# Decoder trunk on one core: delays of the mixer steps chosen anew, and VectorE and ScalarE held behind each weight unit's split

## The chip, the core and the metric

One core of a Trainium2 chip. The metric is the device time of one execution in microseconds (us); smaller is better. The core has TensorE (PE in the profile), VectorE (DVE), ScalarE (ACT), GpSimd (POOL), and SyncE (SP), whose queue here issues most DMAs. Each engine works through its own instructions in the order in which they were written for it, and waits on semaphores for the others.

## The reference

Two layers of a hybrid decoder, for 256 tokens of width 2048, in float32. Of each layer this matters:

```python
proj = rms_norm(h, norm_w[l]) @ w_in[l]
y_a = deltanet_branch(dn_qkv, dn_z, dn_b, dn_a, ...)   # causal conv, SiLU, chunked delta rule, head norm, gate
y_b = hgrn2_branch(hg_q, hg_f, hg_i, ...)              # gated recurrence with one decay per channel, head norm, gate
h = h + concat([y_a, y_b]) @ w_out[l]
h = h + (p[l] @ w_ple_up[l]) * sigmoid(h @ w_ple_gate[l])
```

A final norm follows the second layer. Each branch has eight heads of 128, and the kernel treats them as four groups of two.

## The kernel before

**Weights.** All weight matrices are cut into about 390 units, in the order in which TensorE uses them: per layer the input projection (128 units), the output projection, the gate and the "up" projection. Units 0 to 127 are the input projection of layer 0, units 196 to 323 that of layer 1; unit 196+n of layer 1 corresponds to unit n. A unit comes by one DMA into a `raw` tile (five buffers). ScalarE writes its rounded part `whi` (L451), VectorE the rest, `wlo` = raw - whi (L453): this is the unit's split. `whi` and `wlo` have three buffers each, so the split of unit n needs the products of unit n-3 to be over. TensorE makes twelve matmuls of 128x512 per unit: whi times the high and the low part of the activations, and wlo times the high part (L389 is the helper for all matmuls). Tiles are named by kind, layer and group: `in1hi` is the projection that feeds layer 1's hg branch, and so on.

**The mixers.** Between the units' products, the two branches are computed as Python generators ("jobs"), one for each branch and group (`dn` delta rule, `hg` gated recurrence, `di` the triangular inverses for all dn groups). After the products of each unit, `run_step` calls `tick`, which counts every job down by one and lets those at zero emit their next step: some VectorE and ScalarE operations, a few small matmuls, DMAs. How many units pass between two steps is set by a number for each step, from the table `DELAY`, with exceptions for single groups in `DELAY_AT` (key: kind, group, step; the same for both layers). `yield self.wait("vq")` for dn group 0 waits `d0vq` units.

**What sets the order.** TensorE's instructions keep program order (`keep_in_program_order`). Those of VectorE, ScalarE and SyncE are put in order by the tile scheduler: among the instructions that its own model holds ready, the one that was written first goes first. `ahead(n)` writes the split of unit n+2 before the products of unit n, so a mixer operation that is written after a split can still be scheduled before it, if its operands are ready earlier.

**Names that recur below.** The hg branch needs factors for block sizes 2 to 128, `hg02X2` to `hg02X128` (layer 0, group 2): a VectorE subtraction for each half (L1211, L1213), one ScalarE exponential (L1216), a VectorE product with q (L1223). TensorE uses them in three lots: `hg02pa1` (sizes 1 to 8), `hg02pa16` (16, 32, 64), `hg02pa128`. `hg02fsg`, `hg02qsg`, `hg02k`, `hg02G`, `hg02Gk` are the gates, keys and sums of logarithms that come before them. In the dn branch, `dn10vac` is the convolved v, `dn10pvtr` its transposed copy, brought by a DMA on SP's queue, `dn10R` (L1070) the right-hand side made of it; `dn11zs` copies gate columns out of PSUM (L681). The inverse is built up by block size: `di1T`, `di1pp` (matmul), `di1P` (a ScalarE copy out of PSUM, L848 for size 64), `di1px` (matmul).

Of the kernel before, what the change touches and what calls it, by code (L numbers as in the profile page):

```python
# [8 lines left out]
F32 = mybir.dt.float32  # L9
# [3 lines left out]
AF = mybir.ActivationFunctionType  # L13
ALU = mybir.AluOpType
# [19 lines left out]
def chunk_cols(chunk):  # L34
# [152 lines left out]
def trunk(ctx: ExitStack, tc: tile.TileContext, head, xT, x, pT, W, par, fw, cst, msk, eye, out):  # L187
# [13 lines left out]
    V, S, G = nc.vector, nc.scalar, nc.gpsimd  # L201
# [236 lines left out]
    def prep(n):  # L438
# [11 lines left out]
        for sl in parts:  # L450
            S.activation(hi[:, sl], raw[:, sl], AF.Copy)  # L451
        for sl in parts:
            V.tensor_tensor(lo[:, sl], raw[:, sl], hi[:, sl].bitcast(F32), ALU.subtract)  # L453
# [1175 lines left out]
```

## Time and profile before

| | |
|---|---|
| runs, us | 1198.25, 1199.94, 1200.49 (median 1199.94) |
| the profiled execution, us | 1203.56 |
| its span, us | 1201.6 |
| mean granted TensorE clock | 0.996 |
| TensorE busy | 1183.9 us (99%) |
| VectorE, ScalarE busy | 868.6 (72%), 848.9 (71%) |
| DMA, mean | 221 GB/s |

Busy time is summed over the instructions of an engine. In the view of groups, one row holds all instructions of one line, operation and tile: busy time in all, the mean of one in ns, the engine's idle time just ahead of them, and what ended most of it. In the timeline a row gives start, duration, engine, line, operation, output and inputs, and in brackets the idle time before it with its releaser. A row that ends in xN holds N neighbouring instructions.

### The profile page before, as it was taken

What the parts mean: (1) busy time and instruction counts of PE and PEld (TensorE: products, weight loads), DVE (VectorE), ACT (ScalarE), POOL (GpSimd) and SP (SyncE); (2) the same over time, 40 slices, a digit from 0 to 9 for tenths busy, and PEclk for the clock granted to TensorE, in tenths of its full rate; (3) what the DMA queues carried; (4) which work ended last, traced back from release to release, by engine and by line L of the source; (5) the groups of instructions that cost most, each with busy time, mean ns of one, the idle gap of its engine ahead of it and who ended that gap; (6) DMA issues with size and microseconds to landing.
All of it is one profiled execution on the core that took longest, in us unless ns stands there. A gap on an engine that the chain in (4) does not pass through costs nothing.

```text
span 1201.6 us, 21188 instructions
## 1 busy us (share of the span) xinstructions
PE 1183.9 (99%) x7998; PEld 986.7 (82%) x7998; DVE 868.6 (72%) x1548; ACT 848.9 (71%) x1446; POOL 52.4 (4%) x52
## 2 busy tenths in 40 slices
PE   9999999999999999999999999999999999999997
PEld 8888888978788888888888888878777888888886
DVE  8569896889778655646765789786976786665565
ACT  7587887678787765547866888776876876665453
POOL 0000010001000000000000001000000000000010
PEclk9999999999999999999999999999998999999999
DMA  9589976596666659856978898757574675698562
GB/s 333 198 281 266 300 226 211 170 280 204 198 196 195 182 178 281 248 191 214 277 230 262 240 290 254 217 183 220 184 195 145 200 195 178 212 285 244 182 203 103
DMA packets 178006, 265.88 MB, mean 221 GB/s; under 512 B 107216, under 2 KB 114800, under 8 KB 177648
## 3 DMA queue, kind: packets, MB, share of 16 engines
q1 hardware_dynamic: 153792, 234.48, 64.1%
q10 hardware_dynamic: 24112, 30.06, 7.5%
q8 instruction: 62, 1.02, 0.4%
q14 instruction: 40, 0.33, 0.1%
HBM read 214.94 MB, written 27.02 MB: 201 GB/s over the span
## 4 chain that ended last, share of the span: by engine, by line
PE 66%; DVE 6%; ACT 5%; DMA 4%; issue 3%; SPq 1%; ACTq 0%; POOLq 0%; POOL 0%; DVEq 0%
PE out L389 15%; PE gate L389 14%; PE in1dk L389 7%; PE in1hf L389 7%; PE in1hi L389 6%; PE in0hf L389 3%; PE in0dv L389 3%; DVE wlo L453 2%; PE in1dv L389 2%; PE in0hi L389 2%; PE up L389 2%; ACT whi L451 2%; PE in1dz L389 1%; DMA dn10pvtr<-dn10pvd 1%; SPq L584 1%
## 5 line engine op out<-in xcount | busy, mean ns | idle before, releaser
L453 DVE TENSOR_TENSOR wlo<-raw,whi 128x1024 fp32r<-128x1024 f32 (+2 forms) x393 | 476.3, 1217 | 230.9 <-ACT whi L451 223.3
L451 ACT ACTIVATE whi<-raw 128x1024 fp32r<-128x1024 f32 (+2 forms) x393 | 407.8, 1044 | 204.0 <-PE out L389 59.4
L389 PE MATMUL in1hi<-whi,n1hi 128*128 128x512 f32 x128 | 41.2, 403 | 0.8 <-ACT dn11zs L681 0.8
L389 PE MATMUL in1hf<-whi,n1hi 128*128 128x512 f32 x128 | 40.7, 399 | 1.1 <-ACT hg11zs L681 1.1
L389 PE MATMUL in1dk<-whi,n1hi 128*128 128x512 f32 x128 | 39.8, 392 | 0.0
L389 PE MATMUL in1hi<-whi,n1lo 128*128 128x512 f32 x128 | 39.7, 391 | 0.0
L389 PE MATMUL in1hf<-whi,n1lo 128*128 128x512 f32 x128 | 39.5, 390 | 0.0
L389 PE MATMUL in1dk<-whi,n1lo 128*128 128x512 f32 x128 | 39.5, 390 | 0.0
L389 PE MATMUL gate<-whi,g0hi 128*128 128x512 f32 x128 | 39.4, 389 | 0.0
L389 PE MATMUL gate<-whi,g0lo 128*128 128x512 f32 x128 | 39.4, 389 | 0.0
L389 PE MATMUL in1hi<-wlo,n1hi 128*128 128x512 f32 x128 | 35.7, 391 | 1.8 <-DVE wlo L453 1.8
L389 PE MATMUL in1dv<-whi,n1hi 128*128 128x512 f32 (+1 forms) x128 | 37.4, 384 | 0.0
L389 PE MATMUL in1dv<-whi,n1lo 128*128 128x512 f32 (+1 forms) x128 | 35.8, 372 | 0.0
L389 PE MATMUL gate<-whi,g1lo 128*128 128x512 f32 (+1 forms) x120 | 35.7, 378 | 0.0
L389 PE MATMUL gate<-whi,g1hi 128*128 128x512 f32 (+1 forms) x120 | 35.7, 378 | 0.0
L389 PE MATMUL in1hf<-wlo,n1hi 128*128 128x512 f32 x128 | 35.6, 389 | 0.0
L389 PE MATMUL in1dk<-wlo,n1hi 128*128 128x512 f32 x128 | 35.6, 389 | 0.0
L389 PE MATMUL gate<-wlo,g0hi 128*128 128x512 f32 x128 | 35.5, 389 | 0.0
L389 PE MATMUL gate<-wlo,g1hi 128*128 128x512 f32 (+1 forms) x120 | 32.4, 378 | 0.0
L389 PE MATMUL in1dv<-wlo,n1hi 128*128 128x512 f32 (+1 forms) x128 | 32.3, 370 | 0.0
L389 PE MATMUL in0hi<-whi,n0hi 128*128 128x512 f32 x96 | 30.7, 401 | 0.0
L389 PE MATMUL in0hf<-whi,n0hi 128*128 128x512 f32 x96 | 30.1, 395 | 0.0
(1371 smaller groups left out, 2850.5 us busy)
## 6 DMA issues: line engine op xcount, KB each, us to landing
raw<-W SPq DMA_DIRECT2D x383, 512.0 KB, 4.2
raw<-W SPq DMA_DIRECT2D x7, 544.0 KB, 5.4
h<-x SPq DMA_DIRECT2D x4, 512.0 KB, 4.8
xt<-xT SPq DMA_DIRECT2D x3, 512.0 KB, 7.8
out_dram<-h SPq DMA_DIRECT2D x5, 256.0 KB, 2.4
dn00gall<-dn00d ACTq DMA_DIRECT2D x1, 1024.0 KB, 8.6
di0d<-di0Bt ACTq DMA_DIRECT2D x4, 256.0 KB, 4.5
dn10gall<-dn10d ACTq DMA_DIRECT2D x1, 1024.0 KB, 8.9
```

What stands on the lines that cost most here:

```text
L389: return tc.keep_in_program_order(nc.tensor.matmul(*a, **k))
L451: S.activation(hi[:, sl], raw[:, sl], AF.Copy)
L453: V.tensor_tensor(lo[:, sl], raw[:, sl], hi[:, sl].bitcast(F32), ALU.subtract)
L584: nc.sync.dma_start_transpose(u16(t).rearrange("p (k r) -> p k r", k=c // 128), d.rearrange("(r c) -> r c", c=c))
```

## The change

Two things. First, about 60 of the delays in `DELAY_AT` get other values. Second, a wrapper `Behind` stands in front of VectorE and ScalarE: every operation issued through it is tied, without a semaphore, behind the engine's last "mark", and `prep` sets that mark to the unit's split on this engine. So nothing that is written after the split of unit n can be scheduled ahead of it any more; what was written earlier may still come later. TensorE, GpSimd and SyncE are not wrapped. The instructions are the same in kind and number on every engine; only their order on VectorE, ScalarE and (for a few transfers) SyncE differs, and TensorE's order nearly not: the first half of `hg00pa1` and `hg10pa1` stands one unit earlier, `hg01po` one unit later. As all wrapped operations are issued from the wrapper, their line in the changed kernel is L211.

```diff
 DELAY_AT = {
-    "b0e": 8, "b0g": 3, "b0t": 7,
+    "b0e": 10, "b0g": 3, "b0t": 6,
...
-    "d0D": 6, "d0c": 6, "d0e": 3, "d0k": 4, "d0ke": 7, "d0qe": 3, "d0qt": 2, "d0ssq": 4, "d0v": 7, "d0vt": 3, "d0y": 2, "d0ye": 3, "d0yp": 5, "d0yt": 3, "d0z1": 4,
+    "d0D": 7, "d0c": 6, "d0e": 3, "d0k": 3, "d0ke": 6, "d0q": 8, "d0qe": 3, "d0qt": 2, "d0ssq": 5, "d0v": 7, "d0vq": 5, "d0vt": 3, "d0y": 2, "d0ye": 3, "d0yp": 6, "d0yt": 3, "d0z1": 4,
...
-    "h0a": 1, "h0e": 6, "h0f": 4, "h0o": 9, "h0s2": 3, "h0u16": 1, "h0u64": 2, "h0y": 7, "h0ye": 5, "h0yp": 7, "h0yt": 5,
+    "h0a": 1, "h0a2": 2, "h0e": 5, "h0f": 4, "h0o": 9, "h0s2": 3, "h0u16": 1, "h0u64": 2, "h0y": 4, "h0ye": 5, "h0yp": 8, "h0yt": 5,
...
-    V, S, G = nc.vector, nc.scalar, nc.gpsimd
+    class Behind:
+        def __init__(self, engine):
+            self.engine, self.mark = engine, None
+        def __getattr__(self, name):
+            op = getattr(self.engine, name)
+            def run(*a, **k):
+                i = op(*a, **k)
+                if self.mark is not None:
+                    tc.add_manual_dep(i.ins, self.mark, mybir.DependencyInfo(
+                        mybir.DependencyClass.NoSync, mybir.DependencyReason.DATA), reason="order")
+                return i
+            return run
+
+    V, S, G = Behind(nc.vector), Behind(nc.scalar), nc.gpsimd
...
         for sl in parts:
-            S.activation(hi[:, sl], raw[:, sl], AF.Copy)
+            S.mark = S.activation(hi[:, sl], raw[:, sl], AF.Copy).ins.name
         for sl in parts:
-            V.tensor_tensor(lo[:, sl], raw[:, sl], hi[:, sl].bitcast(F32), ALU.subtract)
+            V.mark = V.tensor_tensor(lo[:, sl], raw[:, sl], hi[:, sl].bitcast(F32), ALU.subtract).ins.name
```

**VectorE, layer 1, where `dn10R` stands.** The number behind `wlo` is the unit; numbers after an underscore are buffers. Before:

```order
L1211 TENSOR_TENSOR hg12X16_9758<-hg12G_9176,hg12Gk_9180 128x16x16 [waits PE_49]
L1213 TENSOR_TENSOR hg12X16_9758<-hg12G_9176 128x16x16
L453 TENSOR_TENSOR wlo294_9585<-raw294_9395,whi294_9584 128x1024 [waits DMAHW2_49,Activation_49]
L514 TENSOR_SCALAR hg12sz_9574<-hg12sz_9574 128x512 [waits Activation_49]
L1070 TENSOR_TENSOR dn10R_9781<-dn10pvtr_9532,invn_7275 128x512 [waits DMAHW1_49]
L1274 TENSOR_TENSOR hg12Ad_9534<-hg12pa1_9535,cs_90 128x128 [waits PE_49]
L453 TENSOR_TENSOR wlo295_9640<-raw295_9452,whi295_9639 128x1024 [waits DMAHW3_49,Activation_49]
L1240 COPY_PREDICATED hg12Ad_9534<-ms_91,hg12pa1_9535 128x64 [waits DVE_49]
L1223 TENSOR_TENSOR hg12X16_9758<-hg12X16_9758,hg12q_9127 128x16x16 [waits Activation_49]
```

and in the changed kernel:

```order
L211 SCALAR_TENSOR_TENSOR dn11vac_9781<-dn11vtr_9509,pr_89,dn11vac_9781 128x254 [waits DVE_49]
L211 TENSOR_TENSOR wlo298_9794<-raw298_9637,whi298_9793 128x1024 [waits DMAHW7_49,PE_49,Activation_49]
L211 SCALAR_TENSOR_TENSOR dn11vac_9781<-dn11vtr_9509,pr_89,dn11vac_9781 128x253 [waits DVE_49]
L211 TENSOR_TENSOR dn10R_9809<-dn10pvtr_9532,invn_7294 128x512 [waits DMAHW1_49]
L211 TENSOR_TENSOR wlo299_9816<-raw299_9693,whi299_9815 128x1024 [waits DMAHW2_49,PE_49,Activation_49]
L211 TENSOR_SCALAR dn11sg_9790<-dn11sg_9790 128x512 [waits Activation_49]
L211 TENSOR_TENSOR hg12X32_9868<-hg12G_9176,hg12Gk_9180 128x8x32
L211 TENSOR_TENSOR hg12X32_9868<-hg12G_9176 128x8x32
L211 TENSOR_TENSOR wlo300_9880<-raw300_9763,whi300_9879 128x1024 [waits DMAHW4_49,PE_49,Activation_49]
```

`dn10R` stood one place behind the split of unit 294, ahead of that of 295; now it stands between those of 298 and 299. The product and the subtractions for `hg12X16` and `hg12X32` have moved too: X16's subtractions from ahead of the split of 294 to behind that of 296.

**VectorE, layer 0, around the splits of units 94 to 97.** Before:

```order
L453 TENSOR_TENSOR wlo93_3191<-raw93_3017,whi93_3190 128x1024 [waits DMAHW5_49,PE_49,Activation_49]
L514 TENSOR_SCALAR dn00sg_3155<-dn00sg_3155 128x512 [waits Activation_49]
L1223 TENSOR_TENSOR hg02X4_3243<-hg02X4_3243,hg02q_2998 128x64x4
L453 TENSOR_TENSOR wlo94_3251<-raw94_3089,whi94_3250 128x1024 [waits DMAHW6_49,PE_49,Activation_49]
L1056 TENSOR_TENSOR dn00vac_3146<-dn00vac_3146,dn00sg_3155 128x512 [waits DVE_49,Activation_49]
L1223 TENSOR_TENSOR hg02X8_3329<-hg02X8_3329,hg02q_2998 128x32x8
L453 TENSOR_TENSOR wlo95_3337<-raw95_3163,whi95_3336 128x1024 [waits DVE_49,DMAHW7_49,PE_49,Activation_49]
L797 COPY_PREDICATED di0Tt_2168<-ms_91,di0px16_3206 32x16x16 [waits PE_49]
L797 COPY_PREDICATED di0Tt_2168<-ms_91,di0px16_3206 32x16x16 x3
```

and in the changed kernel:

```order
L211 TENSOR_TENSOR wlo94_3251<-raw94_3089,whi94_3250 128x1024 [waits DMAHW6_49,PE_49,Activation_49]
L211 COPY_PREDICATED di0Tt_2168<-ms_91,di0px16_3206 32x16x16 [waits PE_49]
L211 TENSOR_TENSOR dn00vac_3146<-dn00vac_3146,dn00sg_3155 128x512 [waits DVE_49,Activation_49]
L211 TENSOR_TENSOR hg02X4_3243<-hg02X4_3243,hg02q_2998 128x64x4 [waits Activation_49]
L211 COPY_PREDICATED di0Tt_2168<-ms_91,di0px16_3206 32x16x16 x3
L211 STREAM_TRANSPOSE di0T32_3302<-di0Tt_2168 32x512 [waits DVE_49] x2
L211 TENSOR_TENSOR hg02X8_3308<-hg02G_3075,hg02Gk_3079 128x32x8
L211 TENSOR_TENSOR hg02X8_3308<-hg02G_3075 128x32x8
L211 TENSOR_TENSOR wlo95_3316<-raw95_3163,whi95_3315 128x1024 [waits DMAHW7_49]
L211 TENSOR_TENSOR wlo96_3389<-raw96_3187,whi96_3388 128x1024 [waits DMAHW1_49,PE_49,Activation_49]
L211 TENSOR_TENSOR hg02X8_3308<-hg02X8_3308,hg02q_2998 128x32x8 [waits Activation_49]
L211 TENSOR_TENSOR wlo97_3452<-raw97_3248,whi97_3451 128x1024 [waits DMAHW4_49,PE_49,Activation_49]
```

Before, the subtractions for `hg02X8` stood ahead of the split of unit 93 and its product ahead of that of 95. Now the subtractions are the last operations ahead of the split of 95, behind two transposes `di0T32`, and the product stands behind the split of 96. TensorE still uses X4 and X8 right after the products of unit 94. `hg02X64`, for `hg02pa16` right after unit 102, has moved in the same way: its exponential stood ahead of `whi99` and now stands behind `whi105`.

**ScalarE, layer 1, between the splits of units 286 and 287.** Before, from the first pass of `dn11sz` on (ahead of it stand `whi286`, two copies out of PSUM, an exponential and six small copies, the same in both kernels):

```order
L513 ACTIVATE dn11sz_9138<-dn11zs_9135 128x512 [waits Activation_49]
L577 DMA dn11vd_9134<-dn11vet_9131 128x512
L451 ACTIVATE whi287_9192<-raw287_9033 128x1024 [waits DMAHW1_49,PE_49]
L520 ACTIVATE dn11sz_9138<-dn11sz_9138 128x512 [waits DVE_49]
L1176 ACTIVATE hg12fsg_9123<-hg12k_9171,tiny_101 128x512 [waits DVE_49]
L521 ACTIVATE dn11sz_9138<-dn11sz_9138 128x512 [waits Activation_49]
```

and in the changed kernel, from the same pass on:

```order
L211 ACTIVATE dn11sz_9138<-dn11zs_9135 128x512 [waits Activation_49]
L211 ACTIVATE hg12fsg_9123<-hg12fsg_9123 128x512 [waits DMAHW5_49]
L211 ACTIVATE hg12qsg_9128<-hg12qsg_9128 128x512
L211 ACTIVATE dn11sz_9138<-dn11sz_9138 128x512 [waits DVE_49]
L211 ACTIVATE hg12fsg_9123<-hg12fsg_9123 128x512 [waits Activation_49]
L211 ACTIVATE dn11sz_9138<-dn11sz_9138 128x512 [waits Activation_49]
L211 ACTIVATE hg12qsg_9128<-hg12qsg_9128 128x512
L211 ACTIVATE hg12fsg_9123<-hg12fsg_9123,lb_112,oml_113 128x256 [waits DVE_49] x2
L211 COPY dn11vet_9131<-dn11vet_9131 128x512
L211 ACTIVATE whi287_9192<-raw287_9033 128x1024 [waits DMAHW1_49,PE_49]
L211 ACTIVATE hg12fsg_9123<-hg12k_9171,tiny_101 128x512 [waits DVE_49]
L211 ACTIVATE hg12q_9127<-hg12q_9127 128x16x16 [waits DVE_49]
```

Nine passes of about half a microsecond stand between this one and `whi287`, where before there was only a DMA issue. The six of `hg12fsg` and `hg12qsg` among them stood ahead of `whi284`, `whi285` and `whi286` before.

24 rows, old and new, of the table DELAY_AT are left out of this document.

## The prediction

> **What bounds the kernel now.** I read the page's first part, then the view of what TensorE waits for, then the timelines of the engines around its longest waits.
>
> ```profile
> PE 1183.9 (99%) x7998; PEld 986.7 (82%) x7998; DVE 868.6 (72%) x1548; ACT 848.9 (71%) x1446; POOL 52.4 (4%) x52
> ...
> L453 DVE TENSOR_TENSOR wlo<-raw,whi 128x1024 fp32r<-128x1024 f32 (+2 forms) x393 | 476.3, 1217 | 230.9 <-ACT whi L451 223.3
> ```
>
> TensorE is busy for 99% of the span. The change takes no instruction away, so only two things can move the time: the few waits that TensorE has, and new ones. VectorE's 28% of idle time is worth nothing by itself; it matters only where an operation that TensorE needs stands behind one that is not ready.
>
> ```profile
> PE di1px L389 <- ACT di1P L848: 2.5, 2, 2.2
> PE in1hi L389 <- DVE wlo L453: 1.8, 1, 1.8
> ...
> PE in1hf L389 <- ACT hg11zs L681: 1.1, 1, 1.1
> PE hg02pa L389 <- DVE hg02X L1223: 1.0, 1, 1.0
> PE in1hi L389 <- ACT dn11zs L681: 0.8, 1, 0.8
> PE hg10pa L389 <- DVE hg10X L1223: 0.6, 1, 0.6
> ```
>
> The columns are us in all, times, longest. The six rows sum to 7.8 us, and five of them lie in layer 1. This is nearly all that a better order could return, but for one thing that hangs on the first row:
>
> ```profile
> 905.58 0.74 PE L389 MATMUL in1dv<-whi,n1hi 128*128 128x512 f32 x2
> ...
> 907.55 1.08 PE L389 MATMUL in1dv<-wlo,n1hi 128*128 128x512 f32 x4
> 910.83 0.30 PE L389 MATMUL di1px<-di1Tt,di1P 64*32 64x64 f32 x2 [2.20 <-ACT di1P L848]
> 911.43 1.87 PE L389 MATMUL di1px<-di1Tt,di1P 64*32 64x64 f32 x62 [0.30 <-ACT di1P L848]
> 913.24 1.22 PE L389 MATMUL in1dv<-whi,n1hi 128*128 128x512 f32 x2
> ...
> 917.67 0.95 PE L389 MATMUL in1dv<-wlo,n1hi 128*128 128x512 f32 x2
> ```
>
> ```profile
> 323.26 1.10 PE L389 MATMUL di0px<-di0Tt,di0P 64*32 64x64 f32 x64
> ```
>
> ```profile
> 914.00:916.00 2.00, 2.00 (x7) 0.50 0.45 158
> ```
>
> The last row is from the table by stretches (busy time, granted clock, DMA share, GB/s): behind the wait of 2.2 us the granted TensorE clock is 0.50. Unit 299, the one from 913.24, takes 5.4 us, unit 298 ahead of it 3.05 (905.58 to 908.63); the 62 small matmuls take 1.87 where 64 take 1.10 in layer 0. The dip costs 2.3 + 0.8 = 3.1 us.
>
> **The change, part by part.** The durations are those of the profiled execution: 1203.56 us, span 1201.6. The three timed runs lie 3.6 us below it (median 1199.94), about the price of the dip; I can't see whether they have it, and count it half.
>
> *(a) `dn10R` moves behind the split of unit 298: gain.* VectorE, then ScalarE, before:
>
> ```profile
> 892.81 0.69 DVE L1070 TENSOR_TENSOR dn10R<-dn10pvtr,invn 128x512 f32<-128x512 f32 x1 [4.87 <-DMA dn10pvtr<-dn10pvd]
> ...
> 893.74 1.22 DVE L453 TENSOR_TENSOR wlo<-raw,whi 128x1024 fp32r<-128x1024 f32 x1
> ```
>
> ```profile
> 903.95 1.22 DVE L453 TENSOR_TENSOR wlo<-raw,whi 128x1024 fp32r<-128x1024 f32 x1
> ```
>
> ```profile
> 900.44 0.64 ACT L1216 ACTIVATE hg12X<-hg12X 128x512 f32<-128x512 f32 x1 [5.01 <-DVE hg12X L1213]
> ...
> 908.08 0.63 ACT L520 ACTIVATE dn11sg<-dn11sg 128x512 f32<-128x512 f32 x1 [0.84 <-DVE dn11sg L514]
> 908.61 1.04 ACT L451 ACTIVATE whi<-raw 128x1024 fp32r<-128x1024 f32 x1
> 909.56 0.61 ACT L521 ACTIVATE dn11sg<-dn11sg 128x512 f32<-128x512 f32 x1
> 910.20 1.18 ACT L848 COPY di1P<-di1pp 64x512 f32<-64x512 f32 x2
> ```
>
> VectorE stood 4.87 us at `dn10R` for its DMA, with the split of 295 (893.74) behind it; ScalarE then stood 5.01 us for a factor that VectorE had not reached, and the copies of `di1P` came out at 910.2 to 911.4, where TensorE wanted them at 908.6. In the new order the same DMA landing (892.8) has until the split of 298, at 903.95 in this trace, so the wait goes. What is late next: `di1P` still stands behind `whi300`, the last `dn11sg` pass and now also the exponential of `hg12X32`. From the start of `whi300` to the end of the second copy that is 1.04 + 0.61 + 0.63 + 1.18 = 3.5 us, less some 0.3 of overlap; TensorE has the `di1pp` lot and one unit in that time, 3.8 us. But `whi300` begins only behind a `dn11sg` pass that waits for VectorE, which works off the six `dn11vac` sums, `dn10R` and two splits first; followed from the end of unit 294 this leaves 0.6 us of the 2.5 (bounds 0 and 2.5). Gain 1.9, and with it the dip, 3.1, counted 1.6.
>
> *(b) Gate passes leave units 262 to 266: gain.* TensorE's waits for `hg11zs` (1.1) and `hg10X` (0.6) fall where ScalarE does the first passes of `hg11fsg` and `hg11qsg` between the same splits; these now stand some six splits later, and the copies out of PSUM come in time. At unit 284 `dn11zs` stood behind two passes that waited for VectorE; they are gone from there: 0.8. Gain 2.5 (bounds 1 and 2.5, as the layer-0 places have no wait to lose).
>
> *(c) `hg02pa1` after unit 94: loss.* PE, VectorE and ScalarE there:
>
> ```profile
> 279.79 1.07 PE L389 MATMUL in0hi<-wlo,n0hi 128*128 128x512 f32 x4
> ...
> 289.45 0.74 PE L389 MATMUL hg02pa<-hg02X 128*32 128x16 f32 x64
> ```
>
> ```profile
> 283.26 1.22 DVE L453 TENSOR_TENSOR wlo<-raw,whi 128x1024 fp32r<-128x1024 f32 x1
> 284.51 1.88 DVE L797 COPY_PREDICATED di0Tt<-ms,di0px 32x256 f32<-32x256 int32 x4
> 286.41 1.43 DVE L802 STREAM_TRANSPOSE di0T<-di0Tt 32x512 f32<-32x512 f32 x2
> 287.88 0.43 DVE L1211 TENSOR_TENSOR hg02X<-hg02G,hg02Gk 128x256 f32<-128x256 f32 x1
> ```
>
> ```profile
> 279.91 0.61 ACT L1216 ACTIVATE hg02X<-hg02X 128x512 f32<-128x512 f32 x1
> ```
>
> Now X4's product, three of the four copies, the transposes, X8's two subtractions, two splits and X8's product follow one another on VectorE: 0.43 + 1.41 + 1.43 + 0.86 + 2.44 + 0.43 = 7.0, less about 0.09 of overlap at each of nine joints: 6.2. X8's exponential (0.61) hides under the splits. The start is set by X4's exponential on ScalarE, which can't come before `whi95`, hence not before unit 92's end (280.8) + 1.04 + 0.63 + 0.61 = 283.1; with the dn00 product ahead of it and ScalarE late from the extra gate passes between `whi90` and `whi91` I come to 285.3. End: 289.3 to 291.5. TensorE wants X8 at 289.45 + 0.3 = 289.8, about 0.5 later if `wlo92` is as late as I find (0.6). Loss 0.6 + 1.2 = 1.8; bounds 0 and 3.
>
> *(d) `hg02X64` behind `whi105`: loss.*
>
> ```profile
> 312.94 1.07 PE L389 MATMUL in0dv<-wlo,n0hi 128*128 128x512 f32 x4
> 313.94 0.91 PE L389 MATMUL hg02pa<-hg02X 128*32 128x64 f32 x64
> ...
> 319.87 0.71 PE L389 MATMUL hg02pa<-hg02X 128*128 128x128 f32 x4 [1.04 <-DVE hg02X L1223]
> ```
>
> `whi105` needs the buffer of unit 102 and can begin some 0.5 before that unit ends, at 313.4; with 1.04, the exponential 0.61 and the product 0.43, X64 is there at 315.4 to 315.6, wanted at 313.94: 1.7. But `hg02pa128` then starts later too, and its present wait of 1.0 shrinks by nearly that much. Net 0.7 (bounds 0.3 and 1.7).
>
> *(e) Units 287 and 288: loss.*
>
> ```profile
> 856.04 1.06 ACT L451 ACTIVATE whi<-raw 128x1024 fp32r<-128x1024 f32 x1
> ...
> 860.44 1.04 ACT L451 ACTIVATE whi<-raw 128x1024 fp32r<-128x1024 f32 x1
> ```
>
> ```profile
> 866.19 2.44 DVE L922 SCALAR_TENSOR_TENSOR dn10vac<-dn10vtr,pr,dn10vac 128x255 f32<-128x255 f32 x6
> ```
>
> `whi286` and `whi287` start 4.4 us apart; nine more passes of about 0.55 (0.63 less overlap) make it 9.3, and two of them wait for `hg12k`, which VectorE has behind four transposes `di1T16` now. TensorE has three units and two small lots for the same stretch, 9.4 us from unit 283's end; `whi286` begins 1.3 us after that end, so `whi287` is about 1.8 late, then `whi288` 0.5 and `wlo288` (behind the six `dn10vac` sums) 1.3. Of these 3.6 the present 1.8 at `wlo` is not new: loss 1.8 (bounds 0 and 3).
>
> *(f) Fuller stretches elsewhere* (VectorE between the splits of 74 and 75, of 38 to 41 and 59 to 62, `hg01X64`): the buffers give TensorE a lead of two units, 5.4 us, less a split of 1.06 and 1.22, so only what exceeds about 4 us of extra work shows. 0.6 (bounds 0 and 2). Moves that keep two splits of lead, and all in the output and gate units, are hidden under the units' matmuls; a stretch without that cover would pay its own surplus.
>
> Sum: -1.9 - 1.6 - 2.5 + 1.8 + 0.7 + 1.8 + 0.6 = -1.1; 1199.94 - 1.1 = 1198.8.
>
> [...]
>
> **Rivals.**
>
> *The clock dips in layer 0 (slower).* The lot `hg02pa1` after unit 94 is made of small matmuls, as `di1px` was. If its wait comes near the 2.2 us that stood ahead of the dip (my upper end is 3), the granted clock falls there, at 3.1 us, while (a) and (b) still gain. It decides from about 2 us of wait. With (c) and (e) at their upper ends: -1.9 - 1.6 - 2.5 + 3 + 3.1 + 1.7 + 3 + 2 = +6.8, 1206.7; at a middle course 1203.5. For it: both lots follow stretches in which ScalarE and VectorE are late at once. Against: 1.8 us at 868 brought no dip.
>
> *The bursts stay under cover (faster).* If (c) and (e) lie near 0 and the dip is in every run, -1.9 - 3.1 - 2.5 + 0.3 + 0.6 = -6.6: 1193.3. For it: in the trace a split is usually there 4 to 5 us ahead, and my walks add every lateness. Against: X64 can't be in time by its place alone.
>
> *`dn10R` was not what held `di1P`.* ScalarE's own passes hold it, 2.5 and the dip stay: -2.5 + 4.9 = +2.4: 1202.3. Against it stands the chain of 4.87 and 5.01 above.
>
> **Chances.** The forecast 0.45 (its own range 1196 to 1201.5), clock dip and slower 0.22, under cover 0.25, `dn10R` 0.08. A measurement here tells 0.2%, 2.4 us. The forecast falls under that 0.16, within it 0.25, above 0.04; the second and third case are wholly on their side; the last is half within, half slower. Faster 0.41, same 0.29, slower 0.30. The range, 1192 to 1205, leaves out the far ends of the two rivals.
>
> **What would show it.** (a) No idle time of 5 us on VectorE ahead of `dn10R`, TensorE's wait for `di1P` under 1 us, granted clock 1 around 914. (b) No rows for `hg11zs`, `hg10X`, `dn11zs`. (c) and (d) New rows: `hg02pa` waiting for `hg02X` two or three times, 3 to 4 us in all. (e) `in1hi` waiting for `whi` or `wlo`, 3 to 4 us. The prediction is wrong if layer 1 keeps its waits, if layer 0 gets none, or if a dip of the clock turns up at another place.

## The result and the profile after

The changed kernel takes 1209.12 us (median of 1207.59, 1208.89, 1209.36 and 1209.81), the kernel before on the same chip 1199.1 (1197.51 to 1200.49). The ratio is 1.0068, 95% interval 1.0039 to 1.0097: slower, and outside the predicted range. The profiled execution has 1207.59 us and a span of 1205.9, 4.3 more than the span of before. Every ratio below is to the kernel before on the same chip; one execution each of `e6_x64_early` (1307.17 us at a mean clock of 0.85) and `e12_hg_only` (1683.68 at 0.655) is left out of its ratio.

What TensorE waits for in the changed kernel (us in all, times, longest):

```profile
PE hg02pa L406 <- DVE hg02X L211: 4.4, 2, 3.2
PE in0hf L406 <- DVE wlo L211: 2.5, 1, 2.5
PE in1hi L406 <- ACT whi L211: 1.6, 1, 1.6
PE in1hf L406 <- DVE wlo L211: 1.3, 1, 1.3
PE gate L406 <- ACT pg L211: 1.2, 1, 1.2
PE warm L406 <- DVE zeros L211: 1.1, 1, 1.1
PE in0hi L406 <- ACT whi L211: 0.8, 1, 0.8
PE in1hi L406 <- DVE wlo L211: 0.6, 1, 0.6
```

None of the six rows of before is left as it was: `di1P`, `hg11zs`, `dn11zs` and `hg10X` are gone, `in1hi` for `wlo` keeps 0.6 of 1.8 us, and the wait for `hg02X` stands at two other places (1.2 for X8, 3.2 for X64) instead of one (1.0 for X128). The other rows are new. Without `warm`, which is the same in both, the rows sum to 12.4 us. Those of before sum to 7.8, and to 8.3 with a seventh that is gone too:

```profile
PE di1px L389 <- issue: 0.5, 1, 0.5
```

That is +4.1. TensorE's busy time is 1183.9 us in both kernels, so the 4.3 us between the two spans are idle time; the 0.2 that are missing are waits too short for a row.

The dip of the granted clock (a stretch at half clock) has moved. It no longer stands at 912 to 918 us. The table by stretches (busy time of PE, PEld, DVE, ACT, POOL, then granted clock, DMA share, GB/s):

```profile
320.00:322.00 2.00, 0.61 (x33) 0.62 (x37) 2.00 (x3) 1.18 (x2) 0.00 (x0) 0.55 0.96 336
322.00:324.00 2.00, 2.00 (x45) 1.77 (x41) 1.79 (x6) 0.76 (x3) 0.00 (x0) 0.50 0.97 328
324.00:326.00 2.00, 2.00 (x7) 1.52 (x6) 0.34 (x1) 1.82 (x6) 0.00 (x0) 0.50 0.98 375
326.00:328.00 2.00, 2.00 (x27) 1.40 (x29) 0.09 (x1) 0.79 (x3) 0.00 (x0) 0.74 0.27 102
...
914.00:916.00 2.00, 2.00 (x69) 1.46 (x69) 1.58 (x4) 1.05 (x2) 0.00 (x0) 1.00 0.83 279
```

It begins at 320.2 (0.55 in the first stretch is 1.8 us at half clock), inside the longest of the new waits, that for `hg02X64` after unit 102. TensorE there:

```profile
317.16 1.07 PE L406 MATMUL in0dv<-wlo,n0hi 128*128 128x512 f32 x4
321.38 1.47 PE L406 MATMUL hg02pa<-hg02X 128*32 128x64 f32 x64 [3.15 <-DVE hg02X L211]
322.79 1.22 PE L406 MATMUL in0dv<-whi,n0hi 128*128 128x512 f32 x2
...
327.13 0.63 PE L406 MATMUL in0dv<-wlo,n0hi 128*128 128x512 f32 x2
```

Unit 103 takes 4.9 us (from 322.79 to 327.69, where the next lot begins) for 2.7, and the 64 small matmuls 1.47 for 0.91: 2.8 us, where the dip of before cost 3.1. So each of the two executions has one dip ahead of the last matmul, of nearly the same price. The medians lie further apart than the spans, because the profiled execution of before (1203.56) lies above its median and that of the changed kernel is the lowest of its four; below, each kernel is compared with runs of before on its own chip.

How X64 comes to be 3.2 us late, on ScalarE:

```profile
315.47 0.64 ACT L211 ACTIVATE dn01sg<-dn01vac 128x512 f32<-128x512 f32 x1 [1.18 <-DVE dn01vac L211]
...
317.49 1.29 ACT L211 ACTIVATE dn01sg<-dn01sg 128x512 f32<-128x512 f32 x2 [0.43 <-DVE dn01sg L211]
318.69 1.04 ACT L211 ACTIVATE whi<-raw 128x1024 fp32r<-128x1024 f32 x1
319.63 0.61 ACT L211 ACTIVATE hg02X<-hg02X 128x512 f32<-128x512 f32 x1
```

and then on VectorE:

```profile
319.77 1.22 DVE L211 TENSOR_TENSOR wlo<-raw,whi 128x1024 fp32r<-128x1024 f32 x1
320.91 0.42 DVE L211 TENSOR_TENSOR hg02X<-hg02X,hg02q 128x256 f32<-128x256 f32 x1
321.25 1.22 DVE L211 TENSOR_TENSOR wlo<-raw,whi 128x1024 fp32r<-128x1024 f32 x1
```

By the estimate of (d) `whi105` could begin 0.5 us before unit 102's end (in the gate units of this trace a split that waits for its buffer starts at 1122.78, 0.9 ahead of the unit's end at 1123.65); it begins 0.5 after it (317.16 + 1.07 = 318.2), since two `dn01sg` passes stand ahead of it, which waited for VectorE. The exponential ends at 320.24, but on VectorE the split of 104 (319.77) stands ahead of its product, which starts 0.7 later; the row at 321.25 is the split of 105. So the chain is held on both engines. The product stands ahead of `wlo105`, and exponential and product are written in one step: hence the tie does not hold the exponential behind `whi105` itself. The scheduler placed it there. That it did so because the subtractions, tied behind `wlo103`, come late is likely, and no run shows it alone.

The second wait, at the split of unit 75. VectorE between the splits of 74 and 75, first and last rows:

```profile
217.76 1.21 DVE L211 TENSOR_TENSOR wlo<-raw,whi 128x1024 fp32r<-128x1024 f32 x1
218.89 0.41 DVE L211 TENSOR_TENSOR di0pr<-di0fx 128x144 f32<-128x144 f32 x1
219.22 0.68 DVE L211 TENSOR_TENSOR_SCAN hg01G<-cs,hg01fsg 128x256 f32<-128x256 f32 x1
...
224.84 0.42 DVE L211 TENSOR_TENSOR hg01X<-hg01G 128x256 f32<-128x256 f32 x1
225.17 1.22 DVE L211 TENSOR_TENSOR wlo<-raw,whi 128x1024 fp32r<-128x1024 f32 x1
```

Sixteen operations of 6.3 us (218.89 to 225.17) stand in a row, none of them waiting (the expectations below count one too many), and TensorE needs `wlo75` 2.5 us before it is there. The two chains that meet here, the inverse's recurrence (`di0pr`, `di0fx`) and the gates of `hg01`, were spread over several units before.

### The profile page after: what moved, and what is told of

Same layout as the page of the kernel before. It is cut to its first block, busy times and chain, and to the rows that moved or that the text cites. A ratio compares the mean times of both kernels' runs of the same rounds, so it can differ in the third digit from the quotient of the medians.

```text
span 1205.9 us, 21181 instructions
## 1 busy us (share of the span) xinstructions
PE 1183.9 (98%) x7998; PEld 986.2 (82%) x7998; DVE 869.7 (72%) x1548; ACT 850.3 (71%) x1446; POOL 63.6 (5%) x52
## 3 DMA queue, kind: packets, MB, share of 16 engines
q8 instruction: 62, 1.02, 0.3%
## 4 chain that ended last, share of the span: by engine, by line
PE 87%; DVE 5%; ACT 3%; DMA 2%; issue 2%; SPq 0%; POOLq 0%; POOL 0%; ACTq 0%; DVEq 0%
PE out L406 14%; PE gate L406 11%; PE in0dk L406 7%; PE in1hf L406 7%; PE in1dk L406 7%; PE in0hf L406 7%; PE in1hi L406 6%; PE in1dv L406 6%; PE in0hi L406 6%; PE in0dv L406 5%; DVE wlo L211 2%; PE up L406 1%; PE in0dz L406 1%; ACT whi L211 1%; DMA raw<-W 1%
## 5 line engine op out<-in xcount | busy, mean ns | idle before, releaser
L211 DVE TENSOR_TENSOR wlo<-raw,whi 128x1024 fp32r<-128x1024 f32 (+4 forms) x401 | 479.3, 1202 | 251.8 <-ACT whi L211 248.1
L211 ACT ACTIVATE whi<-raw 128x1024 fp32r<-128x1024 f32 (+3 forms) x400 | 411.7, 1035 | 245.7 <-PE out L406 68.2
```

Of the source, the lines that this page charges most:

```text
L211: i = op(*a, **k)
```

## The experiments

The theories at first: the tie costs more than it saves, by bursts (many operations in a row between two splits) and by stops at the head of a queue (an operation that is not ready holds ready ones behind it). The rivals: the new delays cost; the dip alone is the difference. The diffs show the main lines of each edit.

**The kernel before again, the new delays alone, the tie alone.**

`e1_before` is the kernel before. Edit of `e2_table` against the changed kernel:

```diff
-    V, S, G = Behind(nc.vector), Behind(nc.scalar), nc.gpsimd
+    V, S, G = nc.vector, nc.scalar, nc.gpsimd
```

`e3_behind` keeps `Behind` and takes `DELAY_AT` from the kernel before.

> The kernel before, unchanged, so that each of its executions has its own clock and span. Theory (the dip of the clock behind di1px is not in every execution): most executions end near 1199 with a clock near 0.999, and one with a clock of 0.996 is about 3 us longer. Rival (the dip is always there): every execution has 0.996, and the times near 1199 have another reason.

> The new delays without the wrapper. In the written order dn10R, hg02X8 and hg02X64 stand where they stood before the change. Theory (the wrapper, not the delays, moves what costs time): 1197 to 1202, with TensorE still waiting about 2 us for di1P and not for hg02pa. Rival (the new delays themselves write the steps too late): 1205 to 1210, hg02pa waiting 3 us or more.

> The old delays with the wrapper. Theory (the wrapper moves the factor tiles behind the splits): 1205 to 1212, TensorE waiting for hg02X and for wlo around unit 75, and no wait for di1P at unit 298, as dn10R stands behind the split of 297 now. Rival (the loss needs the new delays): 1197 to 1202.

Measured, with before at 1202.35 on this chip: `e1_before` 0.999 (0.997 to 1.001), `e2_table` 1196.07, 0.9937 (0.9912 to 0.9961), `e3_behind` 1203.17, 0.9999 (0.9983 to 1.0015). The new delays are no loss. The tie costs some 16 us on them (0.9937 to 1.0068), or some 9 by a second measurement of the new delays (`e16` below, 0.9993). On the old delays it is about even, so the theory for `e3_behind` fell to its rival. That it is even hides a loss and a gain: without `warm`, TensorE's waits in the profile of `e3_behind` sum to 11.6 us, where those of before sum to 8.3, and the mean clock of its runs is 0.998 against 0.996. `e2_table` missed too: it ended below its range, without a wait for `di1P` and with one of 2.6 us for `hg02X128`. The theory for `e1_before` fell: none of its executions had a clock near 0.999. The profile of the kernel before, taken again, differs from the first in the place of the dip. TensorE's waits in `e1_before`:

```profile
PE di1px L389 <- ACT di1P L848: 2.6, 2, 2.3
PE hg02pa L389 <- DVE hg02X L1223: 1.7, 1, 1.7
```

and its stretches behind the second of these waits:

```profile
322.00:324.00 2.00, 2.00 (x8) 1.71 (x9) 0.11 (x1) 1.98 (x5) 0.00 (x0) 0.55 0.24 96
324.00:326.00 2.00, 2.00 (x7) 1.57 (x6) 1.11 (x1) 1.41 (x3) 0.00 (x0) 0.60 0.00 0
```

The wait for `di1P` is there, as long as before, but the dip is not behind it: it follows the wait of 1.7 us for `hg02X128` in layer 0. By the mean granted clock (0.996 over the runs of before on each of the five chips of the experiments) I take it that a dip comes in most executions of before; in the two profiles it stands at different waits.

**Which engine's tie.** `e4_behind_dve` and `e5_behind_act`: the new delays, `Behind` on one engine only.

```diff
-    V, S, G = Behind(nc.vector), Behind(nc.scalar), nc.gpsimd
+    V, S, G = Behind(nc.vector), nc.scalar, nc.gpsimd   # e5: nc.vector, Behind(nc.scalar)
```

> The new delays with the wrapper on VectorE alone; ScalarE's operations are free again. Theory (VectorE's subtractions being placed behind its splits is what makes the factors late): most of the loss stays, 1205 to 1209, hg02pa waits for hg02X 3 to 4 us. Rival (ScalarE's exponentials behind whi are the late step): 1199 to 1203.

> The new delays with the wrapper on ScalarE alone; VectorE's operations are free to be placed early. Theory (the tie on VectorE is what costs, since it puts the subtractions of the factors and whole bursts of gate work behind the splits): within 4 us of the new delays alone, 1195 to 1200, no wait for wlo at unit 75. Rival (either tie alone costs as much): 1205 to 1210.

Measured: 1209.87, 1.0059 (1.0042 to 1.0077), and 1207.78, 1.0048 (1.0025 to 1.0071). Either half costs nearly as much as both, so the theory for `e5` fell to its rival. The same waits appear (`hg02pa` 3.2 and 2.4, `in0hf` for `wlo` 3.0 and, in two parts, 2.1). This fits that an operation held on one engine makes its successor on the other late, but no row here follows such a pair.

**Single operations.** `e6_x64_early`: the changed kernel, X64's step one unit earlier, its use at the same place. `e7_table_u64`: the new delays without the tie, X128's use (`hg02pa128`, `hg12pa128`) one unit later. `e8_dn_r`: the kernel before, `dn00R` and `dn10R` alone written one unit later and tied behind the last split.

```diff
-"h2u16": 1, "h2x64": 2
+"h2u16": 2, "h2x64": 1                      # e6
+"h2u64": 2                                  # e7, added
+i = V.tensor_tensor(R, v4(pv), bc(self.invn, 128), ALU.mult)
+if g == 0: tc.add_manual_dep(i.ins, state["mark"], ...)   # e8, with "d0vq": 5
```

> The whole change, but the X64 factors of group 2 are written one unit earlier and the matmuls that use them wait one unit more, so that TensorE's order is the same and the exponential of hg02X64 stands ahead of whi105. Theory (that exponential behind whi105 makes TensorE's 3.2 us wait for hg02pa, and the dip of the clock hangs on this wait): 4 to 6 us less than the changed kernel, 1202 to 1205, hg02pa waits under 1.5 us, no dip around 322. Rival (the wait is made by the fuller engines in general and only moves): within 2 us of the changed kernel.

> The new delays without the wrapper, and hg02pa128 and hg12pa128 one unit later. Theory (the one long wait that the new delays leave, 2.6 us at hg02pa128, is for a factor that is one unit late): 1 to 3 us less than the new delays alone, 1193 to 1195. Rival (hg02pa128 later makes hg02po and what follows late): no gain, or 1 to 2 us more.

> The kernel before, with dn10R (and dn00R) alone tied behind the last split, one unit later; it stands behind the split of 298 then. Theory (a) of the prediction (VectorE's stop of 4 to 5 us at dn10R is what makes di1P late): no stop there, TensorE's wait for di1P under 1 us, 2 to 5 us faster than before. Rival (ScalarE's own passes hold di1P): the wait of about 2.5 us and the time of before stay.

Measured, before at 1202.22: `e6` 1.0036 (1.0017 to 1.0054); `e7` 0.9964 (0.9945 to 0.9984); `e8` 0.9977 (0.9953 to 1.0002). In `e6` the wait of 3.2 and the dip at it are gone (longest wait for `hg02X` 1.4), which is worth about 4 us against 1.0068, or 5 against 1.0078 of `e9` below, though the intervals overlap or touch; the rest of the loss stays, and a dip stands at 228, at the wait of 2.4 for `wlo75`. In `e8` the stop at `dn10R` and the wait for `di1P` are gone, as (a) had it; a dip follows the wait of 1.8 at unit 288, which had none in the first profile of before. Its gain of some 3 us is not clear of the noise. In `e7` the wait of `hg02pa` is gone, and others of 1.6 (`in1hi` for `wlo`) and 1.5 (`in0hf` for `dn02zs`) stand instead: no gain on `e2`, as its rival said.

**Loosening the tie.** `e9_after` is the changed kernel on the chip of the next three. `e10_lag` sets the mark one unit late; `e11_hg_free` leaves the operations of the hg gates and factors untied, `e12_hg_only` ties these alone.

```diff
-            S.mark = S.activation(hi[:, sl], raw[:, sl], AF.Copy).ins.name
+            s_ = S.activation(hi[:, sl], raw[:, sl], AF.Copy).ins.name     # e10; V alike
+        S.mark, S.last = S.last, s_
...
-                if self.mark is not None:
+                if self.mark is not None and not state["free"]:   # e11: free in HG.f_side, HG.q_side; e12: elsewhere
```

> The changed kernel once more, on the same chip as the three kernels below, so that they can be compared with it. Theory (the tie of the later operations to each split costs some 10 us, which outweighs the gain of the new delays of about 6): ratio to before 1.004 to 1.009, about 1208 where before is 1202; in the profile hg02pa waits for hg02X about 3 us and in0hf for wlo about 2.5 us at the same places as in the first run, since these follow from the order alone. Rival (the loss of the first run belonged to its chip or to where the clock happened to dip): ratio 0.999 to 1.002, and the waits turn up elsewhere.

> The changed kernel with the tie one unit looser: an operation may not be ahead of the split before the last one, so it can pass one split. On ScalarE the exponential of hg02X64 then stands ahead of whi105 again, and on VectorE 8 operations instead of 17 lie between the splits of 74 and 75. Theory (the tie costs by the length of the bursts that it makes between two splits, and by operations put behind a split that is itself waiting for its buffer): most of the cost goes, ratio 0.994 to 1.001 (1195 to 1203 where before is 1202); the wait for hg02X at pa16 goes, and the one of in0hf for wlo75 falls from 2.5 to under 1. Rival (any fixed order between splits and the other operations costs, however loose): ratio 1.003 to 1.007, the sum of TensorE's waits stays above 12 us.

> The changed kernel with the tie left off for the operations of the hg gates and factors on both engines (the passes over hg..fsg and hg..qsg, the exponentials and the products of hg..X), and kept for all others (dn, di, the output units). X64 then stands ahead of whi105 and the stretches between two splits hold at most 8 operations. Theory (it is the hg passes and factors that are bunched, since TensorE waits mainly for hg..X and for splits behind such bunches): most of the cost goes, ratio 0.994 to 1.000 (1195 to 1202). Rival (the bunches of dn and di operations cost as much): ratio 1.002 to 1.006, and the rows of in1hi and in1hf in layer 1 stay at 1.5 us or more.

> The reverse of the kernel before: the tie for the operations of the hg gates and factors alone, all others (dn, di, the output units) as free as in the kernel before; the delays are the new ones. Theory (the bunched hg passes are the cost): ratio 1.002 to 1.007 (1204 to 1210), with waits for hg..X or for splits of over 10 us in all. Rival (dn and di are the cost, or only both together, since a burst between two splits becomes long only where the two kinds meet; between the splits of 74 and 75 this order has 8 operations where the change has 17): ratio 0.994 to 0.999 (1195 to 1201).

Measured, before at 1201.98: `e9` 1210.23, 1.0078 (1.0054 to 1.0101), with the same waits at the same places to 0.1 us but for the one at the gate, which is absent, and with a dip at each of the two longest (from 226.5 and from 322.1); `e10` 0.9995 (0.9981 to 1.0009); `e11` 1.0007 (0.999 to 1.0023); `e12` 0.9995 (0.9976 to 1.0015). One unit of slack takes away 10 us, as the theory had it, though the wait at X64 stays in part (1.1 for `hg02X` at the longest) and that of `in0hf` for `wlo` falls only to 1.7. The theory's expectation for `e12` fell, and so did the one for `e11` by a little: the tied hg operations are not the cost by themselves, and the others are not either. It takes both, as the rival for `e12` had it (its range ended just below, at 0.999), which fits the stretch between 74 and 75, where chains of the two kinds stand between each other. Between `e11` and `e12` two rows tell what the tie of the hg gates is good for. TensorE's waits in `e11`:

```profile
PE in0hf L406 <- ACT hg01zs L211: 1.1, 1, 1.1
PE in1hf L406 <- ACT hg11zs L211: 1.1, 1, 1.1
```

and its ScalarE in layers 0 and 1:

```profile
197.73 0.63 ACT L211 ACTIVATE hg01fe<-hg01fqtr 128x512 f32<-128x512 f32 x1 [4.28 <-DMA hg01fqtr<-hg01fqd]
...
790.30 0.63 ACT L211 ACTIVATE hg11fe<-hg11fqtr 128x512 f32<-128x512 f32 x1 [4.16 <-DMA hg11fqtr<-hg11fqd]
```

In `e12` this operation is tied:

```profile
802.90 0.61 ACT L211 ACTIVATE hg11fe<-hg11fqtr 128x512 f32<-128x512 f32 x1
```

and there is no row for `hg01zs` or `hg11zs`. `hg11fe`, the first pass of the gates, waits for a transposed load. At the head of ScalarE's queue it holds the copies out of PSUM behind it. ScalarE in the kernel before has the same stop:

```profile
784.77 0.63 ACT L516 ACTIVATE hg11fe<-hg11fqtr 128x512 f32<-128x512 f32 x1 [4.06 <-DMA hg11fqtr<-hg11fqd]
```

**The lead of the splits.** `e13_four`: a fourth pair of split buffers, paid for by two other pools. `e14_less`: those pools smaller, three pairs. `e15_table_four`: as `e13` without the tie. `e16_table`: the new delays without the tie, again.

```diff
-    wr = pool("wraw", 5)
-    ws = pool("wsplit", 3)
-    tp = pool("tmp", 6)
+    wr = pool("wraw", 4)      # and WRAW = 4
+    ws = pool("wsplit", 4)    # e14: 3
+    tp = pool("tmp", 4)
```

> The changed kernel with a fourth pair of buffers for the split weights (whi and wlo), so that a split can run one unit earlier, 2.7 us; the memory comes from the raw weights (five buffers to four) and from the temporaries (six to four), which moves some rows on each engine. The bursts between two splits are as long as before (24 and 28 operations at the longest). Theory (the tie costs because a split that waits for its buffer holds what is tied behind it, and the burst that follows is longer than the lead of the splits): with one more unit of lead most of the stops go; ratio 0.992 to 1.000, waits of TensorE under 8 us in all where the changed kernel has 15. Rival (the operations are late by their place, whatever the lead): ratio 1.004 to 1.009, waits of 13 us or more.

> The changed kernel with the smaller pools of the kernel above (four raw weights, four temporaries) but three pairs of split buffers: what the shrinking itself costs. Both theories: near the changed kernel, ratio 1.004 to 1.012 (1207 to 1217); below 1.002 would mean that the gain of the kernel above is not the fourth pair's.

> The new delays without the tie, with four pairs and the smaller pools. Theory (without the tie the two units of lead nearly suffice, TensorE waits 3.8 us in all): the fourth pair gains at most 3 us; ratio 0.990 to 0.998, and the kernel above, with the tie, comes within 0.5% of it. Rival (the tie costs whatever the lead): the kernel above stays 0.8% or more behind it.

> The new delays without the tie once more. Both theories: ratio 0.991 to 0.997 (about 1192 to 1198 where before is 1202), one wait of 2 to 3 us of hg02pa for hg02X, no dip of the clock before the end.

Measured, before at 1200.58: 1.015 (1.012 to 1.018), 1.02 (1.0173 to 1.0227), 1.0117 (1.0091 to 1.0143), and `e16` 1199.7, 0.9993 (0.9972 to 1.0014). All three absolute expectations missed: the smaller pools cost about 1.2% (`e14` against the changed kernel), with new waits all over. What is left is the difference: with four pairs the tie costs 0.33% (`e13` to `e15`), within the 0.5% that the theory gave it and under the rival's 0.8%. There was no run of the new delays with small pools and three pairs, so I count this as pointing to the lead, not as shown.

The surprise is `e16`: the kernel that was 0.994 on one chip is 0.999 on another. The profiled execution of `e16` (1205.12 us) is the slowest of its twelve, that of `e2` (1194.41) the second quickest of its six; so the pair shows how one execution loses time, and does not settle why the medians part. Where the two profiles part in layer 0, VectorE in `e2_table`:

```profile
305.02 0.69 DVE L1070 TENSOR_TENSOR dn00R<-dn00pvtr,invn 128x512 f32<-128x512 f32 x1 [1.87 <-DMA dn00pvtr<-dn00pvd]
...
322.12 0.42 DVE L1223 TENSOR_TENSOR hg02X<-hg02X,hg02q 128x256 f32<-128x256 f32 x1 [1.57 <-ACT hg02X L1216]
```

and in `e16_table`:

```profile
308.04 0.69 DVE L1070 TENSOR_TENSOR dn00R<-dn00pvtr,invn 128x512 f32<-128x512 f32 x1 [3.31 <-DMA dn00pvtr<-dn00pvd]
...
325.13 0.43 DVE L1223 TENSOR_TENSOR hg02X<-hg02X,hg02q 128x256 f32<-128x256 f32 x1 [1.57 <-ACT hg02X L1216]
```

What TensorE waits for in `e16_table`:

```profile
PE hg02pa L389 <- DVE hg02X L1223: 3.6, 1, 3.6
...
PE in1hf L389 <- ACT hg11zs L681: 0.9, 1, 0.9
...
PE hg10pa L389 <- DVE hg10X L1223: 0.5, 1, 0.5
```

The transposed load came 1.4 us later after its issue (SP issues it at 299.02 in the one, 300.60 in the other). Everything behind it on VectorE stands 3.0 us later than in `e2`, 1.6 of it by the later issue; TensorE's matmuls ahead of the wait stand 2.0 later. So `hg02X128` is 3.6 us late for TensorE instead of 2.6, and with 3.6 the dip comes (granted clock 0.50 at 326 to 330), with 2.6 it did not. In layer 1 `hg11fe` stands 4.62 us for its load, in `e2_table` 2.20, and the rows for `hg11zs` and `hg10X` are there again, in the one and not in the other.

**Only six of the operations that wait for a transposed load.** `e17_two_ties` (new delays) and `e18_two_ties_old` (old delays) have no wrapper. `marks` lists the splits.

```diff
+    def behind(i, mark):
+        tc.add_manual_dep(i.ins, mark, mybir.DependencyInfo(
+            mybir.DependencyClass.NoSync, mybir.DependencyReason.DATA), reason="order")
...
+            i = S.activation(e, src, AF.Exp, scale=-1.0)        # hg?1fe; hg?1qsg alike
+            if late: behind(i, marks[-5][0])
...
+            i = V.tensor_tensor(R, v4(pv), bc(self.invn, 128), ALU.mult)
+            if g == 0: behind(i, marks[-1][1])
```

> The new delays, and of the tie only what keeps an operation that waits for a transposed load from standing ahead of a split: hg01fe, hg11fe and their qsg passes (put behind the split two units further on) and dn00R, dn10R (behind the last split). Theory (the tie pays at these operations and costs everywhere else): ScalarE's stop of 2 to 5 us ahead of hg11fe goes, TensorE has no wait for hg11zs, hg10X or di1P; ratio 0.990 to 0.997, and the times lie within 8 us of one another where the new delays alone spread over 12. Rival (the two stops cost nothing by themselves, the difference between the two chips lies elsewhere): ratio 0.994 to 1.000 with the same spread as the new delays alone.

> The kernel before with the same few ties and its old delays. Theory: the waits for di1P (2.5), hg11zs (1.1) and hg10X (0.6) go, 4.2 us, and the dip that stood behind the first mostly comes elsewhere: ratio 0.993 to 0.998 (1193 to 1198 where before is 1201). Rival (TensorE finds its next wait right behind, as hg02X and wlo of unit 288): ratio 0.998 to 1.002.

Measured, before at 1202.38 (1198.97 to 1205.59): `e17` 1194.55 (1193.21 to 1195.38), 0.9931 (0.9914 to 0.9948); `e18` 1194.36 (1193.29 to 1195.74), 0.993 (0.9912 to 0.9949). Both beat both kernels, and their times lie within 2.5 us of one another where those of before spread over 6.6 on this chip. TensorE's waits in `e17`:

```profile
PE hg02pa L389 <- DVE hg02X L1235: 1.2, 1, 1.2
PE warm L389 <- DVE zeros L264: 1.1, 1, 1.1
PE in0dv L389 <- ACT hg02fqet L705: 0.9, 1, 0.9
PE gate L389 <- ACT pg L1395: 0.3, 1, 0.3
```

VectorE at `dn10R` in `e17`:

```profile
899.99 0.68 DVE L1080 TENSOR_TENSOR dn10R<-dn10pvtr,invn 128x512 f32<-128x512 f32 x1
```

and TensorE's waits in `e18`:

```profile
PE di1px L389 <- issue: 1.3, 1, 1.3
PE warm L389 <- DVE zeros L264: 1.1, 1, 1.1
PE in0dv L389 <- ACT hg02fqet L705: 0.9, 1, 0.9
PE in1hi L389 <- DVE wlo L458: 0.9, 1, 0.9
```

No idle time stands ahead of `dn10R` in `e17`, nor of `hg11fe` on ScalarE (787.96). `hg02X128`'s wait is 1.2 or gone, which fits that the stop at `dn00R` had made most of it. The 1.3 of "issue" in `e18` is a gap within one lot that ends with nothing the profile shows. The mean granted clock is 0.997 to 0.999 in all their runs. The two also settle what the new delays are worth: with the few ties, nothing (0.9931 and 0.993).

## Why the prediction was wrong

The steps that failed are (f), the price of the fuller stretches, (d), the price of X64 behind `whi105`, and the halved dip; the first rival named the right mechanism at the wrong place. Part by part the rows of the changed kernel come to -2.5 - 2.5 + 2.0 + 2.2 + 0.4 + 5.0 = +4.6 with no gain from the dip, where the sum had -1.1. That is 5.7 of the 10.3 us between 1198.8 and 1209.12. The rest lies in the base: the sum took rows from an execution of 1203.56 us and began at 1199.94, and the median of the changed kernel lies 1.5 above its profiled execution (together 5.1, less the row of 0.5 that the sum left out). What makes these differences between executions stays open but for the dips (`e9`, at a clock of 0.994, has two where the first profile of the changed kernel, at 0.995, has one).

- **(a) held.** `dn10R` stands at 912.76 behind the split of 298 without a stop, and the wait for `di1P` has no row. `e8_dn_r` shows the wait go by this move alone; its time, some 3 us less, is not clear of the noise.
- **(b) held in its number, and its reason was wrong.** The rows for `hg11zs`, `hg10X` and `dn11zs` are gone. I put the first two down to gate passes between the same splits. They go with the stop of `hg11fe` ahead of these passes: with stops of 4.06, 4.16 and 4.62 us (before, `e11`, `e16`) TensorE waits 0.9 to 1.1 for `hg11zs`, with 2.20 (`e2`) or none (`e12`, `e17`) not at all. The kernel before itself has no stop there in `e1`, and neither row. One run does not fit: a stop of 3.96 in `e7` brings no wait for `hg11zs`, only one of 0.6 for `hg10X`.
- **(c)** The wait for X8 is 1.2 against 1.2, the one of `in0hi` at unit 92 0.8 against 0.6.
- **(d) was mis-sized: 0.7 net against 2.2, and the dip.** X64 was to be 1.7 late, and is 3.2: 1.0 of the difference is ScalarE's lateness at `whi105`, which I had taken from the timeline of before, where no tied `dn01sg` pass stands ahead of it; 0.7 is the split of 104 ahead of the product on VectorE, which I had left out. The present wait of `hg02pa128` (1.0) did go. The dip came at this wait, not at one of `hg02pa1` as the rival had it. `e6` prices the chain at some 4 to 5 us.
- **(e)** `whi287` late by 1.6 against 1.8, `wlo288` by 0.6 against 1.3, `whi288` not at all: 2.2 in all where 3.6 was said, so a net of 0.4 for 1.8.
- **(f) was mis-sized: 0.6 against 5.0** (2.5 at unit 75 in layer 0, 1.3 at its counterpart in layer 1, 1.2 at the gate). It broke its own rule. It said that what exceeds about 4 us of extra work between two splits shows, and it named the stretch between 74 and 75. There the burst is 6.3 us, so the rule gives 2.3; the wait is 2.5. (The subtraction as written, 5.4 - 1.06 - 1.22, leaves 3.1 and not about 4; the 1.06 of ScalarE ran beside the burst here, from 219.38.) I priced all fuller stretches together by feeling, and did not add this one up from its rows. The 1.2 at the gate is of another kind (a split there waits 5.62 us for its raw load) and is absent in `e9`.
- **The dip "counted half".** I could not see whether the three runs of before had it. I take it from the clock that most runs have one: the mean granted clock of before is 0.996 on each of five other chips, that of `e10`, `e17` and `e18`, whose profiles show a dip at the very end alone, 0.998. Taking away one wait did not take the dip away, since it came at another; so the 1.6 us counted as gain were not there.
- **The rivals.** "The clock dips in layer 0" came true in mechanism and sign, not in place, and its 1203.5 to 1206.7 were too low, since they held (d) and (f) at their upper ends of 1.7 and 2. "The bursts stay under cover" is refuted by the waits for X64 and `wlo75`, and by `e10`: one unit of slack is worth 10 us. "`dn10R` was not what held `di1P`" is refuted by `e8`, where the wait goes with the move.

Where the loss came from, then: tied to six operations that wait for a transposed load, and to these alone, the tie gains some 8 us (`e18`, 0.993); laid on all others too it costs some 16 to 18 (`e17` 0.9931 to `e9` 1.0078, on two chips). Loosening it by one unit (`e10`), or leaving it off either for the hg operations or for all others (`e11`, `e12`), gives back 8 to 10. That the loss comes of bursts longer than the lead of the splits, and of chains that stand behind splits on both engines, is shown by rows at unit 75 and at X64, and for X64 by `e6` within its noise; that `e10` gets most of it back fits, but for the other places I infer it.

## What to carry to other kernels

An operation that waits for a load of uncertain landing should not stand ahead of work that others wait for; tying just those few behind the work gave 0.7% here and a steadier time. The same tie laid on everything made bursts of ready operations here: before laying it, add up the rows between two marks and compare the sum with the lead that the buffers give (here 6.3 us against the estimated 4; TensorE waited 2.5), and follow a chain that crosses engines through every split that it comes to stand behind. Where the times of one kernel spread by some 0.5%, the waits of a single profile are one sample: look for the stops that end with a DMA, since these vary (the one at `hg11fe` is 4.06 us in one execution of the kernel before and absent in another, `e1_before`).

## What was not expected of the hardware

**The dip is 3.4 or 6.8 us long in these executions, and which wait brings it changes.** From the granted clock by stretches, its length is 6.8 us in before, in the changed kernel (0.55, 0.50, 0.50, 0.74: 1.8 + 2 + 2 + 1.0) and in `e16`, and 3.4 in `e1` (0.55 and 0.60: 1.8 + 1.6) and in `e8`:

```profile
870.00:872.00 2.00, 2.00 (x55) 1.25 (x59) 2.00 (x5) 1.97 (x3) 0.00 (x0) 0.64 0.44 109
872.00:874.00 2.00, 2.00 (x36) 1.96 (x29) 2.00 (x4) 1.67 (x4) 0.00 (x0) 0.50 0.84 236
```

A wait of 2.3 us (`di1P` in `e1`) and one of 2.6 (`hg02X128` in `e2`) brought none, waits of 1.7 (`hg02X128` in `e1`) and 1.8 (unit 288 in `e8`) did. So in these runs the length of a wait does not tell by itself whether a dip follows; the wait of 1.71 us in `e1` has a lot of 64 small matmuls ahead of it (1.10 us, from 319.02).

The traces of before and of the changed kernel say more on which wait brings the dip. The clock falls at 911.54 us in the one and at 320.19 in the other, for 6.83 us each time. Cut into steps of 3.41 us, half of this dip, from the fall back to 10 us and on to the last matmul, each trace has the least work of TensorE in the step just ahead of the fall: 0.91 us in before, where the next lowest is 1.60 (from 867.16, at the wait of unit 288), and 1.45 in the changed kernel, where the next lowest is 1.59 (from 224.62, at the wait for `wlo75`). So in these two the dip follows the step with the most idle time. How much idle time brings one is not shown: 1.45 and 1.59 lie close together, and at the wait for `wlo75`, which brought none in this execution, a dip stands in `e9` (from 226.5).

**The same transposed load landed 6.0 us after its issue in one execution and 7.4 in another of the same kernel** (`dn00pvtr`: 299.02 to 305.02 in `e2`, 300.60 to 308.04 in `e16`, from the issue to the start of the operation that stood waiting for it). With a consumer at the head of a queue, these 1.4 us made 1.0 us of TensorE wait and a dip in this pair of executions. How much of the difference between 0.994 and 0.999 comes of it is not shown.
